# Delta rule: chunk outputs and the samples' r in 128 by 32 parts of the array

## The chip, the cores and the metric

The kernel runs on one core of a Trainium2 chip. The metric is the device time of one execution in microseconds: before the change 1140.02 us, median of three runs (1139.94 to 1140.26). Engines are named as in the profile: PE (TensorE, matrix products), PEld (its weight loads), DVE (VectorE), ACT (ScalarE), POOL (GpSimd), SP (SyncE, which issues the transfers here).

## What is computed

One layer of a hybrid decoder, in float32, over 256 prompt tokens and 64 sample tokens (8 sequences of 8), 320 together. One projection of the normed input (2048 by 12,416) feeds two branches. Branch B is a gated linear recurrence with 8 heads. Branch A is RWKV-7: 16 heads of 64, each with a 64 by 64 state that follows a delta rule per token:

```
sa  = S kk
S   = S diag(w) - sa (kk * a)^T + v k^T
y_t = S r_t
```

Then come a group norm over each head, a bonus term, gates, two projections (1024 by 2048), a merge by sigmoid gates, and an output projection (2048 by 2048) with a final norm. States and outputs of the prompt and of all sequences are returned.

## The kernel before, in words

**Stages.** A start (30 us) norms and transposes the input. The *planned part* (30 to 702 us) runs the input projection, 128 output columns at a time over 320 tokens, together with both branches, two heads of A (a *pair*, `rwkv`, p = 0 to 7) and one of B (`hgrn`) for each of eight rounds. Then the gates' columns and `proj_a`, `proj_b` (from 702 us), and `w_out` with the norm.

**Weight products.** A weight matrix is divided into two parts of the type fp32r (ACT copies, DVE subtracts), the input too, and three products per 128 by 128 block go into the PSUM tile `mps`. They make the *stream*. All other products are small; most are float32, and the trace shows two records (passes) for each of these.

**The planner.** In the planned part every call is recorded (`Recorder`), linked by what it reads and writes, and issued in an order that a model of the engines gives (`order`, line 209 on). On PE a small product that is ready is put between stream products. Each operation has a cost (line 126 on), so other tile shapes and other counts move everything that follows. Products recorded by `side_by_side` are one *group*: they inherit each other's inputs, so none is issued before all inputs of the group are there. A product on fewer than 128 rows or columns of the array has its own `mode`; the planner stays in a mode while it has work for it (a *visit*), and counts a cost for going in and out. The instructions of the planned part all carry line 1435 in the profile (1441 in the changed kernel), so groups are told apart by tiles.

**The delta rule** (`rwkv`, line 780 on) takes the prompt in four chunks of 64 tokens, both heads in one 128 by 128 block. `arp` holds the decayed kk and r by key, `bk2` and `bk` the decayed keys, `uv` the vectors u (or v) by token, `g2` the masked products of keys with kk and r, `yz`/`ys` the inverted triangles, `s0t` the samples' states (key by value, four tiles of two sequences). Two generators run in turns. `chunks` does for each chunk: the right side (`pr`), u (`pu`), the state's step (`pd`, then `st`), and the output into the PSUM tile `y`: the state times r, and u times the masked products. These are seven products of 128 by 128 with 128 columns, of which the 64 by 64 blocks on the diagonal are used. `samples` does the same for the 64 sample tokens: four products of `s0t` with `arz`, which has kk and r of both heads with zeros elsewhere; a copy of the kk part (`sr0`), turned by a product with the identity and added to `g2` times `uv` (`pr2`); u; the output `py2`, added on DVE to the r part (`sr1`); and the states' step in a visit of four 64 by 64 parts (`pd2`, tile `big` in the profile). `yh` and `yl` are the two fp32r parts of the output, which the group norm reads (`jr_cent`, `jr_mean`).

**The group of branch B** (`pos`, `pg`) is 42 products of 128 rows by 32 columns of the array: eight with 128 columns of moving data, four with 64, the others with 32; one visit a round.

Of the kernel before, what the change touches and what calls it, by code (L numbers as in the profile page):

```python
# [9 lines left out]
F32 = mybir.dt.float32  # L10
F32R = mybir.dt.float32r
# [6 lines left out]
NP_ = 256  # L18
NS = 64
NT = NP_ + NS  # L20
# [274 lines left out]
def hybrid_step(ctx, tc, x_prompt, x_sample, state_rwkv, state_hgrn, state_shift, norm_g, w_in,  # L295
# [4 lines left out]
    V, S, G, T = nc.vector, nc.scalar, nc.gpsimd, nc.tensor  # L300
# [17 lines left out]
    ident = ctile([128, 128], "ident", pool=const)  # L318
# [15 lines left out]
    HS = [slice(0, 64), slice(64, 128)]  # L334
# [29 lines left out]
    def run(gen):  # L364
        for _ in gen:
            pass
# [9 lines left out]
    with tc.tile_pool(name="start", bufs=1) as st, \  # L376
# [167 lines left out]
        with tc.manual_schedule(engines={mybir.EngineType.PE, mybir.EngineType.Activation, mybir.EngineType.DVE,  # L544
# [16 lines left out]
            arp = ctile([128, 5, 2, 2, 64], "arp")  # L561
# [14 lines left out]
            for c_ in range(4):  # L576
                ps = pst.tile([128, 512], F32, name="gps", tag="t")
# [80 lines left out]
            ps = pst.tile([128, 512], F32, name="cps", tag="t")  # L658
# [47 lines left out]
    def ring(pool, tag, shape, bufs, dt, size, clear=False):  # L706

        if (pool.name, tag) not in rings:
            n_ = size or math.prod(shape[1:])
            rings[pool.name, tag] = [0, [pool.tile([128, n_], dt, name=f"{tag}_{j}", tag=f"{tag}_{j}")  # L710
                                         for j in range(bufs)]]
            for t_ in rings[pool.name, tag][1]:
                if clear:
                    G.memset(t_ if dt == F32 else t_.bitcast(F32), 0.0)
        r_ = rings[pool.name, tag]
        t_ = r_[1][r_[0] % len(r_[1])]
        r_[0] += 1
        t_ = t_[:shape[0], :math.prod(shape[1:])]
        if len(shape) == 2:
            return t_  # L720
        names = "abcdef"[:len(shape) - 1]
        return t_.rearrange(f"p ({' '.join(names)}) -> p {' '.join(names)}", **dict(zip(names, shape[1:])))
# [2 lines left out]
             "w1": 384, "w2": 320, "w3": 320, "ks": 128, "ket": 256, "o": NT}  # L725


    CLEAR = {"uB", "uE", "ys", "rhs", "rhs2", "k3", "vm", "w1", "vt", "att", "attc"}
# [9 lines left out]
    def aps(name="aps"):  # L738
        return ring(psa, "a", [128, 512], 3, F32, None)
# [2 lines left out]
        return ring(psb, "b", [128, 512], 2, F32, None)  # L742

    def parts(src, tile_=at):
        hi, lo = tile_("rh", dt=F32R), tile_("rl", dt=F32R)
        S.copy(hi, src)
        V.tensor_sub(lo, src, hi.bitcast(F32))
        return hi, lo
# [31 lines left out]
    def rwkv(p, r, k, vp, za):  # L780
        c = lambda base: cols[:, base + p:base + p + 1]
        v = vp[:, 64:]
# [84 lines left out]
        ps = aps("ps0")  # L867
# [10 lines left out]
                         bk2[:, 4, :, 32 * a_:32 * a_ + 32].rearrange("p j (s i) -> p j s i", i=8),  # L878
                         f[:, None, 8 + 4 * a_:12 + 4 * a_, None].to_broadcast([128, 2, 4, 8]))

        arz = at("arz", (128, 4, 2, 2, 2, 8))
        G.memset(arz, 0.0)
        for h in range(2):
            for s_ in range(2):
                src = arp[HS[h], 4, :, h].rearrange("p x (a b i) -> p b a x i", b=2, i=8)
                G.tensor_copy(arz[HS[s_], :, s_, h], src[:, s_])


        g2 = at("g2", (128, 5, 2, 2, 64))
# [115 lines left out]

        def chunks():
            st_ = None
            py = ring(psy, "y", [128, 512], 1, F32, None)  # L1010
            for ci in range(4):
                cp, c_ = ci // 2, ci % 2
                tk = HS[c_]
                ps = aps("pr")
                T.matmul(ps[:, :128], g2[:, ci, 0].rearrange("p h t -> p (h t)"), uv[:, ci].rearrange("p h v -> p (h v)"), start=True, stop=st_ is None)
                if st_ is not None:
                    T.matmul(ps[:, :128], arp[:, ci, 0].rearrange("p h t -> p (h t)"), st_, start=False, stop=True)
                rt = at("rhs", (128, 2, 64))
                V.tensor_copy(rt[tk, 0], ps[HS[0], 0:64])
                S.copy(rt[tk, 1], ps[HS[1], 64:128])  # L1020
                yield
                pu = aps("pu")
                T.matmul(pu[:, :128], yz[:, cp, c_].rearrange("p h t -> p (h t)"), rt.rearrange("p h t -> p (h t)"), start=True, stop=True)
                V.tensor_scalar(uv[tk, ci, 0], pu[HS[0], 0:64], -1.0, 0.0, op0=ALU.mult, op1=ALU.add)
                S.activation(uv[tk, ci, 1], pu[HS[1], 64:128], AF.Copy, scale=-1.0)
                yield
                pd = aps("pd")
                T.matmul(pd[:, :128], bk[:, ci], uv[:, ci].rearrange("p h v -> p (h v)"), start=True, stop=True)
                sn = at("st", (128, 128), bufs=2)
                fc = f[:, 4 + ci:5 + ci]  # L1030
                if st_ is None:
                    V.tensor_scalar(sn, pd[:, :128], fc, 0.0, op0=ALU.mult, op1=ALU.add)
                else:
                    V.scalar_tensor_tensor(sn, pd[:, :128], fc, sf, op0=ALU.mult, op1=ALU.add)
                po = py[:, 128 * ci:128 * ci + 128]
                if st_ is not None:
                    T.matmul(po, st_, arp[:, ci, 1].rearrange("p h t -> p (h t)"), start=True, stop=False)
                T.matmul(po, uv[:, ci].rearrange("p h v -> p (h v)"), g2[:, ci, 1].rearrange("p h t -> p (h t)"), start=st_ is None, stop=True)
# [12 lines left out]
            so = at("so", (64, 2, 64))  # L1051
            for h in range(2):
                S.copy(so[:, h], ps[HS[h], 64 * h:64 * h + 64])
            Y.dma_start(p_rwkv[0, 0, 2 * p:2 * p + 2].rearrange("h v k -> v h k"), so)
            yield


        def samples():
            ps = aps("psr")
            for sp in range(4):  # L1060
                T.matmul(ps[:, 64 * sp:64 * sp + 64], s0t[:, sp], arz[:, sp].rearrange("p b h x i -> p (b h x i)"),
                         start=True, stop=True)

            sr0, sr1 = at("sr0", (128, 2, 64)), at("sr1", (128, 64))
            for h in range(2):
                p4 = ps[HS[h], :256].rearrange("p (s h x i) -> p h x s i", h=2, x=2, i=8)[:, h]
                V.tensor_copy(sr0[HS[h]].rearrange("p h (s i) -> p h s i", i=8),
                              p4[:, 0:1].to_broadcast([64, 2, 8, 8]))
                S.copy(sr1[HS[h]].rearrange("p (s i) -> p s i", i=8), p4[:, 1])
            yield  # L1070
            ps = aps("pr2")
            T.matmul(ps[:, :128], sr0.rearrange("p h t -> p (h t)"), ident, start=True, stop=False)
            T.matmul(ps[:, :128], g2[:, 4, 0].rearrange("p h t -> p (h t)"), uv[:, 4].rearrange("p h v -> p (h v)"), start=False, stop=True)

            uh = at("uh", (128, 128), tag="s0t")
            for a_ in range(2):
                S.copy(uh[64 * a_ + 32:64 * a_ + 64], uv[64 + 32 * a_:96 + 32 * a_, 4].rearrange("p h v -> p (h v)"))
            rhs = at("rhs2", (128, 2, 64))
            V.tensor_copy(rhs[0:64, 0], ps[HS[0], 0:64])
            S.copy(rhs[0:64, 1], ps[HS[1], 64:128])  # L1080
# [26 lines left out]
            T.matmul(py[:, :128], uv[:, 4].rearrange("p h v -> p (h v)"), g2[:, 4, 1].rearrange("p h t -> p (h t)"), start=True, stop=True)  # L1107
# [4 lines left out]
            yield  # L1112
# [11 lines left out]
            yield  # L1124

        run(together(chunks(), samples()))


        ps = aps("pyc")
# [487 lines left out]
```

## Time and profile before

| | |
|---|---|
| runs | 1140.02 us (1139.94 to 1140.26) |
| profiled execution | 1139.92 us, of which span 1138.2 us |
| PE / PEld / DVE / ACT / POOL busy | 1122.0 / 1087.7 / 766.8 / 700.7 / 179.8 us |
| granted clock of PE | 0.998 |
| read from HBM, written | 148.53 MB, 9.81 MB |

A row of a group reads: line, engine, operation, tile written <- tiles read, rows*columns of the array, moving data, type, count; then busy us, mean ns of one, and idle time of the engine before them. Matmuls are pipelined and overlap in the records; their durations don't add up to the time that they take. A row of the timeline has start and duration in us, and ends with how many records were put together in it. A wait's row has its sum in us, how often, and the longest.

### The profile page before, as it was taken

How to read it: one execution, taken by the hardware profiler on the slowest of the kernel's cores; microseconds unless marked ns; L12 is line 12 of the kernel's file. 1: busy time of each engine (PE TensorE's matmuls, PEld its weight loads, DVE VectorE, ACT ScalarE, POOL GpSimd, SP SyncE). 2: the span in 40 equal slices, each digit the busy share in tenths (PEclk: the TensorE clock that was granted, in tenths of full speed). 3: DMA queues.
4: the chain of work that ended last, by engine and by line, in shares of the span. 5: the costliest groups of instructions: out<-in, count | busy, mean ns of one | idle time of the engine just before them, and what ended most of it. 6: DMA issues, size and time to landing. Idle time of an engine off the chain costs nothing.

```text
span 1138.2 us, 21837 instructions
## 1 busy us (share of the span) xinstructions
PE 1122.0 (99%) x8312; PEld 1087.7 (96%) x8312; DVE 766.8 (67%) x1634; ACT 700.7 (62%) x1612; POOL 179.8 (16%) x385
## 2 busy tenths in 40 slices
PE   7999999999999999999999999999999999999997
PEld 6999999999999999999999999999999999988886
DVE  8878788787887887888778877444444444437532
ACT  6667767777678677678667777444444444435422
POOL 9531132122221411311312200000000000000000
PEclk9999999999999999999999999999999999999999
DMA  6744544535435445345436345555555555587512
GB/s 182 192 114 112 154 115 129 150 95 146 132 100 154 130 114 144 106 111 159 123 96 168 99 122 145 155 148 149 149 149 149 150 149 153 151 272 258 161 38 93
DMA packets 283101, 159.76 MB, mean 140 GB/s; under 512 B 22893, under 2 KB 273264, under 8 KB 282356
## 3 DMA queue, kind: packets, MB, share of 16 engines
q1 hardware_dynamic: 282996, 158.37, 48.7%
q8 instruction: 65, 1.06, 0.4%
q14 instruction: 40, 0.33, 0.1%
HBM read 148.53 MB, written 9.81 MB: 139 GB/s over the span
## 4 chain that ended last, share of the span: by engine, by line
PE 98%; DVE 1%; POOL 0%; ACT 0%; issue 0%; ACTq 0%; DVEq 0%; POOLq 0%
PE mps L1435 42%; PE a L1435 12%; PE mps L359 6%; PE mps L360 6%; PE mps L361 6%; PE b L1435 3%; PE po L1518 3%; PE po L1519 3%; PE po L1520 3%; PE ppb L359 2%; PE ppa L359 2%; PE ppb L360 2%; PE ppa L360 2%; PE ppb L361 2%; PE ppa L361 2%; PE po L1524 1%
## 5 line engine op out<-in xcount | busy, mean ns | idle before, releaser
L1435 PE MATMUL mps<-hhi,whi 128*128 128x320 f32 x1088 | 345.4, 317 | 0.0
L1435 PE MATMUL mps<-hlo,whi 128*128 128x320 f32 x1088 | 345.3, 317 | 0.0
L1435 PE MATMUL mps<-hhi,wlo 128*128 128x320 f32 x1088 | 343.8, 316 | 0.0
L1435 PEld LDWEIGHTS mps<-hhi,wlo 128*128 128x128 f32 x1088 | 204.9, 188 | 2.4 <-issue 1.5
L1435 PEld LDWEIGHTS mps<-hlo,whi 128*128 128x128 f32 x1088 | 205.0, 188 | 1.4 <-issue 0.8
L1435 PEld LDWEIGHTS mps<-hhi,whi 128*128 128x128 f32 x1088 | 204.9, 188 | 1.1 <-issue 0.4
L349 ACT CAST whi<-raw 128x1024 fp32r<-128x1024 f32 x88 | 92.4, 1050 | 162.8 <-PE mps L360 107.3
L350 DVE TENSOR_TENSOR wlo<-raw,whi 128x1024 fp32r<-128x1024 f32 x88 | 107.9, 1226 | 125.0 <-ACT whi L349 124.8
L1435 ACT CAST whi<-raw 128x1024 fp32r<-128x1024 f32 x134 | 140.4, 1048 | 66.3 <-PE mps L1435 65.4
L1435 DVE TENSOR_TENSOR wlo<-raw,whi 128x1024 fp32r<-128x1024 f32 x134 | 166.6, 1243 | 18.1 <-ACT whi L1435 16.7
L359 PE MATMUL mps<-hhi,whi 128*128 128x320 f32 x448 | 138.4, 309 | 0.0
L360 PE MATMUL mps<-hlo,whi 128*128 128x320 f32 x448 | 138.4, 309 | 0.0
L361 PE MATMUL mps<-hhi,wlo 128*128 128x320 f32 x448 | 138.4, 309 | 0.0
L359 PEld LDWEIGHTS mps<-hhi,whi 128*128 128x128 f32 x448 | 84.1, 188 | 0.0
L360 PEld LDWEIGHTS mps<-hlo,whi 128*128 128x128 f32 x448 | 84.1, 188 | 0.0
L361 PEld LDWEIGHTS mps<-hhi,wlo 128*128 128x128 f32 x448 | 84.1, 188 | 0.0
L1507 DVE TENSOR_TENSOR wlo<-raw,whi 128x1024 fp32r<-128x1024 f32 x32 | 38.7, 1223 | 39.0 <-ACT whi L1506 39.0
L1506 ACT CAST whi<-raw 128x1024 fp32r<-128x1024 f32 x32 | 33.5, 1053 | 49.0 <-PE po L1523 32.0
L1518 PE MATMUL po<-whi,mhi 128*128 128x512 f32 x128 | 50.1, 391 | 0.7 <-DVE gbt L1475 0.7
L1519 PE MATMUL po<-whi,mlo 128*128 128x512 f32 x128 | 50.0, 391 | 0.0
L1520 PE MATMUL po<-wlo,mhi 128*128 128x512 f32 x128 | 50.0, 391 | 0.0
L359 PE MATMUL ppa<-yah,whi 128*128 128x320 f32 x128 | 39.6, 309 | 0.0
(428 smaller groups left out, 2268.6 us busy)
## 6 DMA issues: line engine op xcount, KB each, us to landing
raw<-in_w_in_dram SPq DMA_DIRECT2D x194, 512.0 KB
raw<-in_w_out_dram SPq DMA_DIRECT2D x32, 512.0 KB
raw<-in_proj_a_dram SPq DMA_DIRECT2D x16, 512.0 KB
raw<-in_proj_b_dram SPq DMA_DIRECT2D x16, 512.0 KB
s<-in_state_hgrn_dram SPq DMA_DIRECT2D x8, 512.0 KB
out_dram<-s SPq DMA_DIRECT2D x8, 512.0 KB
s<-in_state_rwkv_dram SPq DMA_DIRECT2D x8, 256.0 KB
out_dram<-s SPq DMA_DIRECT2D x8, 256.0 KB
```

The costliest lines, as they stand in the source:

```text
L349: S.copy(hi[:, ks], raw[:, ks])
L350: sub.tensor_sub(lo[:, ks], raw[:, ks], hi[:, ks].bitcast(F32))
L359: T.matmul(dst, hi[:, q, :], xhi[:, k, :], start=(k == 0), stop=False)
L360: T.matmul(dst, hi[:, q, :], xlo[:, k, :], start=False, stop=False)
L361: T.matmul(dst, lo[:, q, :], xhi[:, k, :], start=False, stop=(k == nk - 1))
L1435: o.fn(*o.args, **o.kw)
L1506: S.copy(hi, raw)
L1507: V.tensor_sub(lo, raw, hi.bitcast(F32))
L1518: T.matmul(pt, h, hi, start=first, stop=False)
L1519: T.matmul(pt, l, hi, start=False, stop=False)
L1520: T.matmul(pt, h, lo, start=False, stop=end)
L1524: T.matmul(pt, h, lo, start=False, stop=end)
```

## The change

It makes the same sums in other places.

- The zero-padded `arz` becomes two tiles: `az` has kk of the samples, by head and half of the tokens, for use as the stationary operand, and `rz` has r. POOL fills them with eight copies a pair; the zeros are set once, when the tiles are made (`CLEAR`).
- The samples' right side is made in one group of twelve products, each 128 rows by 32 columns of the array with 64 columns of moving data: four parts (head, half of the tokens), and for each of them two with the states and one with `g2` and `uv`. `sr0`, `sr1`, the turn by the identity and `py2` are gone.
- The chunks keep their states (`st` has four buffers), and the outputs of all chunks and of the samples are made after both generators, in one group of 48 products into the tile `y`, 128 rows by 32 columns each: 32 with 64 columns (the samples' u among them) and 16 with 16 columns (states times `rz`). The four parts are head and half of its 64 value rows, so no block off the diagonal is made.
- `yh` and `yl` are made by one copy and one subtraction over 320 tokens instead of three of each. `uh` is made later, in the buffer of `rhs2`; `s0t` is kept to the last visit. Branch B's `rh` takes the buffer of `vm`.

```diff
-    CLEAR = {..., "vt", "att", "attc"}
+    CLEAR = {..., "vt", "att", "attc", "az", "rz"}
...
-        hi, lo = tile_("rh", dt=F32R), tile_("rl", dt=F32R)
+        hi, lo = tile_("rh", tag="rh" if tile_ is at else "vm", dt=F32R), tile_("rl", dt=F32R)
...
-        arz = at("arz", (128, 4, 2, 2, 2, 8))
-        G.memset(arz, 0.0)
+        az = at("az", (128, 2, 2, 96))
+        rz = at("rz", (128, 4, 2, 2, 8))
         for h in range(2):
             for s_ in range(2):
-                src = arp[HS[h], 4, :, h].rearrange("p x (a b i) -> p b a x i", b=2, i=8)
-                G.tensor_copy(arz[HS[s_], :, s_, h], src[:, s_])
+                own = arp[HS[h], 4, :, h]
+                G.tensor_copy(az[HS[s_], h].rearrange("p a (e f) -> p a e f", f=48)[:, :, :, 8 * s_:8 * s_ + 8],
+                              own[:, 0].rearrange("p (a e b i) -> p a e b i", a=2, e=2, b=2)[:, :, :, s_])
+                G.tensor_copy(rz[HS[s_], :, h, s_], own[:, 1].rearrange("p (a b i) -> p a b i", b=2, i=8)[:, :, s_])
...
         def chunks():
-            py = ring(psy, "y", [128, 512], 1, F32, None)
...
-                sn = at("st", (128, 128), bufs=2)
+                sn = at("st", (128, 128), bufs=4)
...
-                po = py[:, 128 * ci:128 * ci + 128]
-                if st_ is not None:
-                    T.matmul(po, st_, arp[:, ci, 1]..., start=True, stop=False)
-                T.matmul(po, uv[:, ci]..., g2[:, ci, 1]..., start=st_ is None, stop=True)
                 st_ = sn
+                states.append(sn)
...
-            for h in range(2):
-                t4 = lambda t_: t_[HS[h], :NP_].rearrange("p (c t) -> p c t", t=64)
-                y4 = py.rearrange("p (c h t) -> p c h t", c=4, h=2)[HS[h], :, h]
-                S.copy(t4(yh), y4)
-                V.tensor_sub(t4(yl), y4, t4(yh).bitcast(F32))
...
         def samples():
             ps = aps("psr")
-            for sp in range(4):
-                T.matmul(ps[:, 64 * sp:64 * sp + 64], s0t[:, sp], arz[:, sp]..., start=True, stop=True)
-            sr0, sr1 = at("sr0", (128, 2, 64)), at("sr1", (128, 64))
-            for h in range(2):
-                p4 = ps[HS[h], :256].rearrange("p (s h x i) -> p h x s i", h=2, x=2, i=8)[:, h]
-                V.tensor_copy(sr0[HS[h]]..., p4[:, 0:1].to_broadcast([64, 2, 8, 8]))
-                S.copy(sr1[HS[h]]..., p4[:, 1])
-            yield
-            ps = aps("pr2")
-            T.matmul(ps[:, :128], sr0..., ident, start=True, stop=False)
-            T.matmul(ps[:, :128], g2[:, 4, 0]..., uv[:, 4]..., start=False, stop=True)
+            work = []
+            for step in range(3):
+                for h in range(2):
+                    for a_ in range(2):
+                        l_, r_ = (az[:, h, a_, 32 * step:32 * step + 32], s0t[:, 2 * a_ + step, 64 * h:64 * h + 64]) \
+                            if step < 2 else (g2[:, 4, 0, h, 32 * a_:32 * a_ + 32], uv[:, 4, h])
+                        o_ = 64 * h + 32 * a_
+                        work.append(((ps[o_:o_ + 32, :64], l_, r_), dict(start=step == 0, stop=step == 2)))
+            side_by_side(work)
...
-            py = aps("py2")
-            T.matmul(py[:, :128], uv[:, 4]..., g2[:, 4, 1]..., start=True, stop=True)
-            for h in range(2):
-                V.tensor_add(sr1[HS[h]], py[HS[h], 64 * h:64 * h + 64], sr1[HS[h]])
-            S.copy(yh[:, NP_:], sr1)
-            V.tensor_sub(yl[:, NP_:], sr1, yh[:, NP_:].bitcast(F32))
...
         run(together(chunks(), samples()))
+        py = ring(psy, "y", [128, 512], 1, F32, None)
+        work = []
+        parts4 = [(h, 64 * h + 32 * w, w) for h in range(2) for w in range(2)]
+        for ci in range(5):
+            cols_ = slice(64 * ci, 64 * ci + 64)
+            if 0 < ci < 4:
+                for h, o_, w in parts4:
+                    work.append(((py[o_:o_ + 32, cols_], states[ci - 1][:, o_:o_ + 32], arp[:, ci, 1, h]),
+                                 dict(start=True, stop=False)))
+            for h, o_, w in parts4:
+                work.append(((py[o_:o_ + 32, cols_], uv[:, ci, h, 32 * w:32 * w + 32], g2[:, ci, 1, h]),
+                             dict(start=ci in (0, 4), stop=ci < 4)))
+        for sp in range(4):
+            for h, o_, w in parts4:
+                t_ = NP_ + 16 * sp
+                work.append(((py[o_:o_ + 32, t_:t_ + 16], s0t[:, sp, o_:o_ + 32], rz[:, sp, h]...),
+                             dict(start=False, stop=sp == 3)))
+        side_by_side(work)
+        S.copy(yh, py[:, :NT])
+        V.tensor_sub(yl, py[:, :NT], yh.bitcast(F32))
```

How it moves instructions on PE is shown at three places of the last pair. The names: `a_`, `b_` and `y_` are PSUM tiles, `s_0_519` and `s_0_520` branch B's states, `w`, `o`, `ket`, `ks` its decayed queries and keys, `st` the chunks' states. First, PE of the kernel before, in the middle of the chunks:

```order
L1435 MATMUL a_488<-fd_516,jr_sum 128x256
L1435 MATMUL a_487<-rhs_0_510,ys_502 128x128
L1435 MATMUL b_523<-vm_538,k_0_537 128x512
L1435 MATMUL a_486<-uv_495,g_0_501 128x128
L1435 MATMUL a_486<-st_511,arp 128x128
L1435 MATMUL y_506<-arp,st_511 128x128
L1435 MATMUL a_488<-fd_516,jr_sum 128x256
L1435 MATMUL a_487<-g_0_501,uv_495 128x128
```

The output of a chunk (`y_506`) stands beside the next chunk's right side, and the last row is the samples' output `py2`, both on the whole array, between other small products. In the changed kernel, PE after the last chunk of the same pair:

```order
L1441 MATMUL a_487<-uv_495,bk_504 128x128
L1441 MATMUL y_519<-g_0_502,uv_495 32x64 x4
L1441 MATMUL y_519<-arp,st_512 32x64 x4
L1441 MATMUL y_519<-g_0_502,uv_495 32x64 x4
L1441 MATMUL y_519<-arp,st_513 32x64 x4
L1441 MATMUL y_519<-g_0_502,uv_495 32x64 x4
L1441 MATMUL y_519<-arp,st_514 32x64 x4
L1441 MATMUL y_519<-g_0_502,uv_495 32x64 x8
L1441 MATMUL y_519<-rz_501,s0t_497 32x16 x16
L1441 MATMUL mps<-hhi,wlo 128x320
```

All outputs of the pair now stand here as one block of 48 products, behind the last state's product, with the stream on both sides; so it is in each of the eight pairs. The third place is the visit for the samples' right side, PE of the changed kernel, same pair:

```order
L1441 MATMUL b_523<-s_0_520,qz 32x128 x8
L1441 MATMUL b_524<-w_0_529,w_0_521 32x32 x8
L1441 MATMUL b_524<-w_0_528 32x32 x8
L1441 MATMUL b_524<-o_531 32x32 x8
L1441 MATMUL b_524<-ket_532 32x32 x4
L1441 MATMUL b_524<-ks_534,s_0_533 32x64 x4
L1441 MATMUL b_524<-w_0_529,w_0_521 32x32 x2
L1441 MATMUL a_487<-s0t_497,az_500 32x64 x8
L1441 MATMUL a_487<-uv_495,g_0_502 32x64 x4
```

The last two rows are the twelve new products; here, and in the fourth pair, they stand in one visit with branch B's group, in the other six pairs by themselves. The states' visit (`big`) stands in one visit with branch B's in four pairs of the changed kernel and in three before. The variance's product (`jr_mean`) of the last pair has two more stream products ahead of it than before.

More of the change, by code (lines that the diff above doesn't have):

```diff
@@ L725, in hybrid_step @@
              "w1": 384, "w2": 320, "w3": 320, "ks": 128, "ket": 256, "o": NT}
-    CLEAR = {"uB", "uE", "ys", "rhs", "rhs2", "k3", "vm", "w1", "vt", "att", "attc"}
+    CLEAR = {"uB", "uE", "ys", "rhs", "rhs2", "k3", "vm", "w1", "vt", "att", "attc", "az", "rz"}
     def at(name, shape=(128, NT), tag=None, bufs=1, dt=F32):
@@ L1003, in rwkv @@
         yl = at("yl", tag="rl", dt=F32R)
+        states = []
         def chunks():
             st_ = None
-            py = ring(psy, "y", [128, 512], 1, F32, None)
             for ci in range(4):
@@ L1034, in chunks @@
                     V.scalar_tensor_tensor(sn, pd[:, :128], fc, sf, op0=ALU.mult, op1=ALU.add)
-                po = py[:, 128 * ci:128 * ci + 128]
-                if st_ is not None:
-                    T.matmul(po, st_, arp[:, ci, 1].rearrange("p h t -> p (h t)"), start=True, stop=False)
-                T.matmul(po, uv[:, ci].rearrange("p h v -> p (h v)"), g2[:, ci, 1].rearrange("p h t -> p (h t)"), start=st_ is None, stop=True)
                 st_ = sn
+                states.append(sn)
                 if ci < 3:
@@ L1059, in samples @@
             ps = aps("psr")
-            for sp in range(4):
-                T.matmul(ps[:, 64 * sp:64 * sp + 64], s0t[:, sp], arz[:, sp].rearrange("p b h x i -> p (b h x i)"),
-                         start=True, stop=True)
-            sr0, sr1 = at("sr0", (128, 2, 64)), at("sr1", (128, 64))
-            for h in range(2):
-                p4 = ps[HS[h], :256].rearrange("p (s h x i) -> p h x s i", h=2, x=2, i=8)[:, h]
-                V.tensor_copy(sr0[HS[h]].rearrange("p h (s i) -> p h s i", i=8),
-                              p4[:, 0:1].to_broadcast([64, 2, 8, 8]))
-                S.copy(sr1[HS[h]].rearrange("p (s i) -> p s i", i=8), p4[:, 1])
-            yield
-            ps = aps("pr2")
[L1072 to L1077, printed above, removed]
+            work = []
[7 more added lines that the diff above has]
+            side_by_side(work)
             rhs = at("rhs2", (128, 2, 64))
-            V.tensor_copy(rhs[0:64, 0], ps[HS[0], 0:64])
-            S.copy(rhs[0:64, 1], ps[HS[1], 64:128])
+            V.tensor_copy(rhs[0:64, 0], ps[HS[0], :64])
+            S.copy(rhs[0:64, 1], ps[HS[1], :64])
             yield
@@ L1105, in samples @@
             yield
-            py = aps("py2")
-            T.matmul(py[:, :128], uv[:, 4].rearrange("p h v -> p (h v)"), g2[:, 4, 1].rearrange("p h t -> p (h t)"), start=True, stop=True)
-            for h in range(2):
-                V.tensor_add(sr1[HS[h]], py[HS[h], 64 * h:64 * h + 64], sr1[HS[h]])
-            S.copy(yh[:, NP_:], sr1)
-            V.tensor_sub(yl[:, NP_:], sr1, yh[:, NP_:].bitcast(F32))
-            yield
+            uh = at("uh", (128, 128), tag="rhs2")
+            for a_ in range(2):
+                S.copy(uh[64 * a_ + 32:64 * a_ + 64], uv[64 + 32 * a_:96 + 32 * a_, 4].rearrange("p h v -> p (h v)"))
             for a_ in range(2):
@@ L1126, in rwkv @@
         run(together(chunks(), samples()))
+        py = ring(psy, "y", [128, 512], 1, F32, None)
[13 more added lines that the diff above has]
+                t_ = NP_ + 16 * sp
+                work.append(((py[o_:o_ + 32, t_:t_ + 16], s0t[:, sp, o_:o_ + 32], rz[:, sp, h].rearrange("p b i -> p (b i)")),
+                             dict(start=False, stop=sp == 3)))
+        side_by_side(work)
+        S.copy(yh, py[:, :NT])
+        V.tensor_sub(yl, py[:, :NT], yh.bitcast(F32))
         ps = aps("pyc")
```

## The prediction, made before the changed kernel ran

> **What bounds the kernel now.** I read the page's busy table first, then the chain, then the stages.
>
> ```profile
> span 1138.2 us, 21837 instructions
> PE 1122.0 (99%) x8312; PEld 1087.7 (96%) x8312; DVE 766.8 (67%) x1634; ACT 700.7 (62%) x1612; POOL 179.8 (16%) x385
> PE 98%; DVE 1%; POOL 0%; ACT 0%; issue 0%; ACTq 0%; DVEq 0%; POOLq 0%
> 230.00:330.00 100.00, 100.00 (x815) 98.42 (x814) 82.65 (x208) 74.10 (x196) 23.41 (x49) 1.00 0.45 124
> 530.00:630.00 100.00, 99.69 (x810) 97.50 (x809) 82.63 (x202) 70.29 (x181) 23.89 (x53) 1.00 0.47 128
> ```
>
> The last two rows are stages of the planned part: window, its length, then busy time of PE, weight loads, DVE, ACT, POOL, the granted clock, the DMA share and GB/s. PE has no gap, its clock is 1.00, DVE is busy for 83 of 100 us. PE alone decides here: an instruction saved on PE is time saved, and one saved elsewhere is not. But "busy" is no price, because matmuls overlap. The price of a product is by how much it pushes the next start, and that is read from the timeline of PE. This is the last head pair, around its samples (columns: start, duration, instruction, count):
>
> ```profile
> 662.58 0.31 PE L1435 MATMUL mps<-hhi,whi 128*128 128x320 f32 x1
> 662.73 1.00 PE L1435 MATMUL a<-arz,s0t 128*128 128x64 f32 x8
> 663.56 0.44 PE L1435 MATMUL a<-rhs,yz 128*128 128x128 f32 x2
> ...
> 663.99 0.31 PE L1435 MATMUL mps<-hhi,wlo 128*128 128x320 f32 x1
> ...
> 664.58 0.31 PE L1435 MATMUL mps<-hhi,whi 128*128 128x320 f32 x1
> 664.81 0.65 PE L1435 MATMUL b<-s,qz 128*32 128x128 f32 x16
> 665.27 0.31 PE L1435 MATMUL b<-w,w 128*32 128x32 f32 x16
> ...
> 665.67 0.20 PE L1435 MATMUL b<-ket 128*32 128x32 f32 x1
> ...
> 665.77 0.30 PE L1435 MATMUL b<-ks,s 128*32 128x64 f32 x6
> 665.86 0.24 PE L1435 MATMUL b<-w,w 128*32 128x32 f32 x4
> 666.03 0.41 PE L1435 MATMUL mps<-hlo,whi 128*128 128x320 f32 x1
> 666.28 0.38 PE L1435 MATMUL a<-ident,sr 128*128 128x128 f32 x2
> 666.50 0.27 PE L1435 MATMUL b<-ident,es 128*64 128x128 f32 x1
> 666.61 0.39 PE L1435 MATMUL a<-uv,g 128*128 128x128 f32 x2
> 666.83 0.39 PE L1435 MATMUL a<-uv,bk 128*128 128x128 f32 x2
> 667.05 0.39 PE L1435 MATMUL y<-g,uv 128*128 128x128 f32 x2
> 667.20 0.39 PE L1435 MATMUL mps<-hhi,wlo 128*128 128x320 f32 x1
> 667.43 0.31 PE L1435 MATMUL mps<-hhi,whi 128*128 128x320 f32 x1
> ```
>
> Each float32 product stands as two records (passes). The stream of weight products (mps) runs at one per 0.147 us: 663.99 to 664.58 are four. The four products of `arz` run from 662.73 to 663.56, 0.83 us. `ident,sr` takes 666.28 to 666.50, `uv,g` 666.61 to 666.83: 0.22 us each. `y<-g,uv` runs from 667.05; one stream product starts inside it (667.20) and the next at 667.43, so 0.38 less 0.147, 0.23 us.
>
> **Removed.** How many such products there are is in the groups of PE (count, then busy us, mean ns of one):
>
> ```profile
> L1435 PE MATMUL y<-g,uv 128*128 128x128 f32 x64 | 12.4, 275 | 0.0
> L1435 PE MATMUL y<-arp,st 128*128 128x128 f32 x48 | 9.3, 275 | 0.0
> L1435 PE MATMUL a<-arz,s0t 128*128 128x64 f32 x64 | 8.1, 267 | 0.0
> L1435 PE MATMUL a<-uv,g 128*128 128x128 f32 x80 | 15.5, 275 | 0.0
> L1435 PE MATMUL a<-g,uv 128*128 128x128 f32 x16 | 3.1, 274 | 0.0
> L1435 PE MATMUL a<-ident,sr 128*128 128x128 f32 x16 | 3.1, 273 | 0.0
> ```
>
> By pair these are four and three products into `y`, four of `arz`, one of `sr`, one of `g,uv` into `py2`, and of the ten records of `uv,g` the two of the samples (the other eight are the chunks' and stay). So ten products of 128 columns go at 0.22, 2.20 us, and the four of `arz` at 0.83: 3.03 us a pair, **24.2 us** over eight. The busy column would promise 39.1 us (12.4 + 9.3 + 8.1 + 3.1 + 3.1 and a fifth of 15.5); the rest of that lies under neighbours.
>
> **Added: passes of 128 by 32 parts.** The trace has this form in branch B's visit. Sixteen passes with 128 columns take 664.81 to 665.27, 28.75 ns each. 46 passes with 32 columns take 665.27 to 665.67, 8.7 ns each. Six with 64 columns take 665.77 to 665.86, 15 ns each; half of 28.75 is 14.4. I take 14.5 ns for 64 columns. The ends are 8.7, the row below it, and 28.75, the row above. For 16 columns there is no row: I take 8.7, what 32 columns cost, since fewer columns can't cost more; the other end is half of it.
>
> The last visit has 32 products with 64 columns and 16 with 16, that is 64 and 32 passes: 0.93 + 0.28 = 1.21 us. The visit for r has 12 products with 64 columns, 24 passes: 0.35 us.
>
> **Added: going in and out.** Branch B's visit: the stream would have gone on at 664.58 + 0.147 = 664.73, the first pass starts at 664.81. The last four passes start at 665.86 and take 0.03; the stream starts at 666.03, but its next instruction comes at 666.28, 0.25 later instead of 0.147. In and out are 0.08 + 0.24, 0.32 us. The state's visit of four 64 by 64 parts, in an earlier pair, gives the same:
>
> ```profile
> 186.46 0.30 PE L1435 MATMUL mps<-hlo,whi 128*128 128x320 f32 x1
> 186.70 0.66 PE L1435 MATMUL a<-big,s0t 64*64 64x256 f32 x8
> 187.29 0.41 PE L1435 MATMUL mps<-hhi,wlo 128*128 128x320 f32 x1
> 187.54 0.31 PE L1435 MATMUL mps<-hhi,whi 128*128 128x320 f32 x1
> ```
>
> From 186.46 + 0.147 to 187.54 - 0.147 are 0.79 us; eight passes with 256 columns at twice 28.75 are 0.46; 0.33 is left. I take 0.33 for a visit, with 0.08 (the way in alone) and 0.45 (a third more, an estimate) as ends.
>
> By the order of the changed kernel the last visit stands alone in all eight pairs: 8 x (1.21 + 0.33) = 12.3 us. The visit for r stands alone in six; in the fourth and the last pair it is joined to branch B's visit of the same form, and pays no way in or out: 8 x 0.35 + 6 x 0.33 = 4.8 us. The state's visit joins branch B's in four pairs now, in three before; the forms differ, so I count 0.2 of 0.33 saved. Added: 12.3 + 4.8 - 0.2 = **16.9 us**.
>
> **Other engines.** DVE loses six instructions a pair and ACT four; both lie under the stream and are worth nothing. POOL loses a memset and four copies and gets eight:
>
> ```profile
> L1435 POOL COPY arz<-arp x32: 231/268/1135, 62.3 to 623.5; 64x64 f32<-64x64 f32 x32
> L1435 POOL MEMSET arz<- x8: 305/311/312, 37.0 to 573.6; 128x256 f32 x8
> ```
>
> Eight at 0.27 (half the elements each, so at most that) less four and 0.31 are 0.8 us a pair more. Behind them on POOL stand the first blocks `yz` of the inverse, so that chain starts up to 0.8 us later; the stream of weight products covers it. If that cover were gone, it would be 6 us in all. No DMA is added or moved.
>
> **Waits.** A visit is issued as one block and waits for all of its inputs: the last one for the state after the third chunk, u of the fourth and the samples' u. Behind a late input stands the whole weight stream. Against this, what PE waited for in this stage, of everything the planner has placed, is one row:
>
> ```profile
> PE a L1435 <- DVE st L1435: 0.3, 1, 0.3
> ```
>
> I take 0 for the sixteen visits; 0.46 each would cost the whole gain (7.3 / 16).
>
> The outputs of the last pair now come out in one piece after the last chunk, with the norm and the projections behind them. Room there:
>
> ```profile
> L1455 ACT CAST yah<-ya x4: 712/717/724, 696.5 to 699.1; 128x640 fp32r<-128x640 f32 x4
> L1456 DVE TENSOR_TENSOR yal<-ya,yah x4: 817/822/825, 697.5 to 700.0; 128x640 fp32r<-128x640 f32 x4
> L359 PE MATMUL ppa<-yah,whi x128: 309/309/309, 709.3 to 1008.0; 128*128 128x320 f32 x128
> ```
>
> The last split ends at 700.8, PE asks for it at 709.3: 8.5 us. In the order the variance's product of the last pair stands two stream products later than before, 0.3 us. Nothing.
>
> **Sum.** 24.2 - 16.9 = 7.3 us. The profiled execution took 1139.92 us (span 1138.2 and 1.7 around it), 0.1 below the runs' median of 1140.02. 1139.92 - 7.3 = 1132.6; I say **1132.5 us**.
>
> **Rivals.** (1) *A pass with 64 columns costs more than in branch B's visit*, 20 to 25 ns, because here nearly all passes have 64 and in that visit only eight do, among passes with 32. There are 8 x (64 + 24) = 704: 5.5 ns more are 3.9 us, 10.5 more 7.4: 1136.5 to 1140.0. For it: six passes are little to read a pitch from. Against it: 128 columns at 28.75.
>
> (2) *A pass has a floor whatever its columns*, 28.75 ns by the nearest row with long moving data. The 120 passes of a pair then cost 3.45 us, with the ways in and out 27.6 + 4.6 - 0.2 = 32.0 us against 24.2: 1147.7, slower. It decides from about 20.6 ns a pass (24.2 - 4.4 = 19.8 us over 960). Against it stand 46 passes at 8.7 ns. The Trainium skill, page "TensorE: Matmul & The Clock Gate", section "Wait — 56ns, not 53.3ns?", states such a floor: start-to-start never under about 25 ns however small N is. By it the 960 passes would be 24.0 us and the time 1139.9 + 24.0 + 4.4 - 24.2 = 1144.1, slower. The trace disagrees with it for passes that go to different column groups: 8.7 ns.
>
> (3) *The visits wait.* The weight stream stands behind a visit whose inputs come late; at 0.9 us for each of sixteen, 14.4 us, 1147, slower; from 0.46 each there is no gain left. For it: the planner works with costs of its own, and the last visit's inputs come off three engines. Against it: the 0.3 us above, which is all for eight pairs of small products.
>
> (4) *The parts don't overlap where they accumulate.* Two or five products add into one place here; branch B's tiles are single products. A pass that had to wait for the end of the one before it (some 0.22 us) at about nine places a pair would cost 16 us: 1148. Against it: the two passes of one product already add into one place, and pass each other at that pitch.
>
> **How the numbers follow.** A gain of 4.4 to 11 us (1129 to 1135.5): 0.80. (1), with a gain of 0 to 4.4: 0.11. (2): 0.02. (3): 0.05. (4): 0.02. The range goes from 1129.5, where the passes with 64 columns cost 11 ns (2.5 us less) and a few old stalls go, to 1136.5, where they cost 20; that leaves out some 0.17. What this kernel's measurement can tell from no change is about 0.2%, 2.3 us. Faster by more: 0.80 and 0.08 of (1), 0.88. Within it: 0.04. Slower: (2), (3) and (4) with little else, 0.08.
>
> **What would show it.** In the timeline of the changed kernel: the last visit's 96 passes start within 1.2 us and the next stream product is running 0.3 us after; the visit for r takes 0.35 us. The groups of `arz`, `sr` and `y` at 128 by 128 are gone. The planned part, which ends near 702 us, ends near 695; what comes after takes as long as before. The forecast is wrong if the 64-column passes start over 20 ns apart, or if PE's waits in this stage sum to more than 3 us.

## The result, and the profile after

The changed kernel takes 1133.64 us (median of six runs, 1133.14 to 1134.63), the kernel before 1139.97 beside it: 6.3 us less, ratio 0.9945 (95% interval 0.9932 to 0.9958). The forecast was 1132.5, range 1129.5 to 1136.5. The profiled execution took 1133.88 us, 6.0 less than that of before.

The page of the changed kernel, and the rows of the stream's last kind (first and last start):

```profile
span 1132.1 us, 23282 instructions
PE 1110.7 (98%) x9048; PEld 1072.6 (95%) x9048; DVE 754.8 (67%) x1586; ACT 691.3 (61%) x1580; POOL 193.9 (17%) x411
L1441 PE MATMUL mps<-hhi,wlo x1088: 302/309/502, 29.6 to 695.6; 128*128 128x320 f32 x182
```

PE has more records (9048 for 8312) and is busy for less time. The planned part ends near 696 instead of 702 us (the prediction had 695). The last visit of the last pair, in the timeline of PE:

```profile
677.63 0.31 PE L1441 MATMUL mps<-hlo,whi 128*128 128x320 f32 x1
677.77 0.38 PE L1441 MATMUL a<-uv,bk 128*128 128x128 f32 x2
678.09 0.32 PE L1441 MATMUL y<-g,uv 128*32 128x64 f32 x8
678.22 0.29 PE L1441 MATMUL y<-arp,st 128*32 128x64 f32 x8
...
678.78 0.41 PE L1441 MATMUL y<-g,uv 128*32 128x64 f32 x16
679.00 0.47 PE L1441 MATMUL y<-rz,s0t 128*32 128x16 f32 x32
679.40 0.41 PE L1441 MATMUL mps<-hhi,wlo 128*128 128x320 f32 x1
679.65 0.27 PE L1441 MATMUL a<-ident,st 128*128 128x128 f32 x1
```

64 passes with 64 columns start between 678.09 and 679.00: 14.2 ns each. The 32 passes with 16 columns run from 679.00; the stream's product after them is there at 679.40, with the way out. After `uv,bk` (0.22 from 677.77) the first pass comes 0.1 later. In all, 677.99 to 679.65 less 0.147 are 1.51 us; the prediction had 1.54. The visit for r in the first pair:

```profile
92.24 0.31 PE L1441 MATMUL mps<-hhi,whi 128*128 128x320 f32 x1
92.48 0.43 PE L1441 MATMUL a<-s0t,az 128*32 128x64 f32 x16
92.73 0.29 PE L1441 MATMUL a<-uv,g 128*32 128x64 f32 x8
92.95 0.42 PE L1441 MATMUL mps<-hlo,whi 128*128 128x320 f32 x1
93.21 0.49 PE L1441 MATMUL b<-ident,i 128*128 128x128 f32 x3
```

From 92.39 (92.24 + 0.147) to 93.21 less 0.147 are 0.67 us, for a predicted 0.68. What did not come as predicted are the waits. These are PE's in the planned part of the changed kernel, as the profile lists them; the kernel before had one row there, the 0.3 us that the prediction quotes:

```profile
PE a L1441 <- POOL fd L1441: 1.7, 1, 1.7
PE a L1441 <- DVE ast L1441: 1.0, 1, 1.0
```

The list leaves out short waits. To see the whole of the planned part, I took the times between stretches of undisturbed stream and split them by the prices: stream and whole-array products (0.147 a stream product, 0.1105 a float32 pass), what a visit takes beyond that, and the rest as waits (us; the later rows are experiments told below):

```
kernel                         stream and whole array   visits   waits   sum
before                                          639.7     29.2     2.4  671.4
changed                                         614.9     46.3     4.5  665.8
only the outputs in parts                       625.6     40.8     2.2  668.6
only the samples' r in parts                    636.1     33.9     2.0  672.1
outputs twice in one visit                      614.9     70.2     2.5  687.7
outputs twice, apart                            614.9     58.5     5.5  678.9
outputs of 128 columns                          614.9     54.4     2.4  671.7
two buffers for fd                              614.9     49.5     1.3  665.7
two buffers, at most 64 products a visit        614.9     47.5     1.3  663.8
the same, 30 stream products apart              614.9     45.7     1.5  662.2
one buffer, 64 products, 30 apart               614.9     46.4     5.3  666.6
```

24.8 us of whole-array products are gone (forecast 24.2), 17.1 us of visits came (16.9), and the waits grew by 2.1 us (forecast 0): the planned part is 5.6 us shorter. In this count the wait for `fd` makes 1.9 us, that for `ast` 1.1, and all other waits together are 0.9 less than before.

The wait for `ast` is not the change's doing. The start was 0.86 us shorter in this profile than in that of before (the first eight records of `tps<-ident,xt` took 0.71 us for 1.11), so PE came to this product 0.86 us earlier and had to wait for its input. The last experiment, which leaves the change out, has the shorter start and a wait for `ast` too. `w_out` took 0.4 us longer: its first product starts 6.4 us earlier than before, its last 6.0. So the 6.0 us between the two profiles are 5.6 of the planned part and 0.86 of the start, less 0.4 of `w_out`.

### The profile page after: what moved, and what is told of

Read it like the earlier page. It is cut to its first block, busy times and chain, and to the rows that moved or that the text cites. A ratio compares the mean times of both kernels' runs of the same rounds, so it can differ in the third digit from the quotient of the medians.

```text
span 1132.1 us, 23282 instructions
## 1 busy us (share of the span) xinstructions
PE 1110.7 (98%) x9048; PEld 1072.6 (95%) x9048; DVE 754.8 (67%) x1586; ACT 691.3 (61%) x1580; POOL 193.9 (17%) x411
## 4 chain that ended last, share of the span: by engine, by line
PE 89%; DMA 3%; DVE 3%; issue 3%; ACT 1%; POOL 1%; ACTq 0%; SPq 0%; POOLq 0%; DVEq 0%
PE mps L1441 40%; PE a L1441 11%; PE mps L360 6%; PE mps L361 6%; PE mps L359 6%; PE b L1441 3%; DMA raw<-in_w_out_dram 2%; PE po L1526 2%; PE po L1524 2%; PE po L1525 2%; PE ppb L360 2%; PE ppa L361 2%; PE ppa L360 2%; PE ppa L359 2%; PE ppb L359 2%
```

## The experiments

**One group at a time.** First, the samples' right side as before, the outputs in parts:

```diff
-        az = at("az", (128, 2, 2, 96))
+        arz = at("arz", (128, 4, 2, 2, 2, 8))
...
-            side_by_side(work)
+            # four products with arz, sr0, its turn by ident, g2 times uv
```

> One of the two groups undone: the samples' right side is made as before (four products with arz, the turn by the identity, g2 times uv, all on the whole array), the group of 48 output products stays. Theory (PE's time is the sum of what its products and visits occupy): against the kernel before, 8 x 8 x 0.22 = 14.1 us of whole-array outputs go, 8 x 1.21 = 9.7 come, and by the order there are 18 visits instead of 13, 5 x 0.33 = 1.7: 1137 to 1138 us, so the group of outputs alone gains some 2.5 us and the group for r the larger rest (4 us). Rival (the groups don't matter, the new order of the planner does): anything between 1132 and 1140, with no relation to the sum. Rival (a pass with 64 columns costs 20 to 25 ns): 1140 to 1143.

1136.47 us (1136.30 to 1136.82), ratio 0.9970 (0.9959 to 0.9982): 3.4 us below before, where the sum gave 2.7, and 0.5 below the range expected. The start is the shorter one here too (0.84 us); the planned part alone is 2.8 us shorter. Then the other way round, the outputs on the whole array and the twelve products for r kept:

```diff
-        rz = at("rz", (128, 4, 2, 2, 8))
+        arz = at("arz", (128, 4, 2, 2, 8))
...
-        side_by_side(work)
+            # seven products into y in chunks(); in samples() four with arz, and py2
```

> The other group undone: outputs of chunks and samples as before on the whole array, the group of twelve for the samples' right side stays. The states times r then need four whole-array products of 32 columns again. Theory: against the kernel before, two products of 0.22 a pair go (3.5 us), 8 x 0.35 = 2.8 come, and by the order there are 18 visits instead of 13 (1.7 us): about 1141 us, no gain at all, if a whole-array product of 32 columns takes the 0.21 us that one of 64 takes; if it takes in proportion to its columns, 3.3 us less, 1137.7. The gain of the change is then not the sum of its halves: the four products of arz go only when both groups are there. Rival (each group is worth its half): about 1137.

1140.65 us, ratio 1.0008 (0.9999 to 1.0017): no gain, as the sum said with 0.21 us for a whole-array product of 32 columns. Its rows:

```profile
L1442 PE MATMUL a<-arz,s0t 128*128 128x32 f32 x64 | 7.8, 265 | 0.0
L1442 PE MATMUL a<-s0t,az 128*32 128x64 f32 x128 | 3.8, 223 | 0.0
```

There are 64 passes of `arz` again, half as wide and nearly as long (7.8 us for 8.1). The halves are worth 3.4 and -0.8 us and the whole 6.3: with one group alone the four products of `arz` stay, and only both together free PE of them. Without the start and the waits, by the first two columns of the table, the halves are worth 2.5 and -1.1 us and the whole 7.7, for sums of 2.7, -1.0 and 7.3. The rival, a new order of the planner with no relation to the sum, would not give that.

**The passes.** The group of 48 twice in one visit:

```diff
-        side_by_side(work)
+        side_by_side(work + work)
```

> The group of 48 output products is issued twice in one visit, with the same result: the visit's passes alone are doubled, not its way in and out. Theory: 64 passes at 14.3 ns and 32 at 9 are 1.21 us a pair, 9.7 in all, and two more visits by the order (0.6): 1143 to 1145 us. Rival (a pass with 64 columns costs 20 ns or more): 1146 or more. Rival (a floor of 25 to 29 ns for every pass): 1153 to 1156.

1155.66 us, ratio 1.0142 (1.0128 to 1.0156). The theory missed by over 10 us. The number lies in the range of the rival with a floor of 25 to 29 ns for every pass, but the timeline of PE shows no such floor. In the second pair:

```profile
197.90 0.32 PE L1441 MATMUL y<-g,uv 128*32 128x64 f32 x8
...
199.76 0.44 PE L1441 MATMUL y<-g,uv 128*32 128x64 f32 x16
199.98 0.29 PE L1441 MATMUL y<-rz,s0t 128*32 128x16 f32 x13
203.54 0.36 PE L1441 MATMUL y<-rz,s0t 128*32 128x16 f32 x19 [3.27 <-issue]
203.83 0.42 PE L1441 MATMUL mps<-hlo,whi 128*128 128x320 f32 x1
```

The first 160 passes start within 2.1 us, up to 199.98, at the pitch of the changed kernel (128 at 14.2 ns and 32 at 9 ns). 13 more follow, and then PE stands for 3.3 us with nothing to wait for (`issue`). The waits of this kind in this kernel:

```profile
PE y L1441 <- issue: 8.0, 4, 3.3
PE b L1441 <- issue: 1.5, 1, 1.5
```

Three of the eight visits had no stop. They last 2.47, 2.49 and 2.63 us up to the next product on the whole array, where the changed kernel's take 1.31: there the second copy cost 1.2 to 1.3 us, as expected (1.21). Of the 23.9 us that the table's visits hold more than the changed kernel's, 9.7 are these passes, 0.6 two more visits and 9.5 the stops of the list. Most of the rest, 3 us by an estimate, are two stretches of some 3.5 us behind a stop, in which a stream product took 0.267 us for 0.147 (see the last section).

At the time of the stop instructions were being loaded. The trace's records of PE's instruction queue have one transfer of 16,384 bytes for some 256 instructions; those around the stop, with the number of PE's instructions (passes and weight loads) that started since the transfer before:

```
transfer, us from start    PE instructions since the one before
181.21 to 182.34           285
186.92 to 188.10           241
200.96 to 201.89           509
205.09 to 205.96            50
```

With stream products 256 instructions last 19 us (two for each 0.147 us). A visit uses as many in under 2 us, and in no kernel here do two transfers start less than 3.4 us apart. The stop above ends 1.65 us after the transfer that ends at 201.89, and so it is with all ten stops of this kind in the traces here: PE goes on 1.3 to 1.7 us after such a transfer is complete. That made a new theory, *a burst of short instructions uses them up faster than they come*, and two tests. The first has as many instructions in a longer visit, with 128 columns of moving data in 28 of the 32 products that had 64:

```diff
-            cols_ = slice(64 * ci, 64 * ci + 64)
+            wide = 128 if ci < 4 else 64
+            cols_ = slice(64 * ci, 64 * ci + wide)
...
```

> As many instructions as in the changed kernel, but 28 of the 48 output products get 128 columns of moving data instead of 64 (the second half is overwritten by the next chunk's product or not read), so that the visit lasts longer. In the kernel with the outputs twice, PE stopped inside the long visits for 1.4 to 3.4 us with nothing to wait for in the profile, 3.4 us while one 16 KB block of instructions was being fetched. Theory (PE runs out of instructions: a burst of short ones uses them up faster than the next block comes): a longer visit with the same instructions costs its passes alone, 56 x 14.3 ns x 8 = 6.4 us more than the changed kernel, 1139.5 to 1140.5, and no stop over 1 us. Rival (PE stops when it has been in a visit for long): stops as in the kernel with the outputs twice, 1146 or more.

1139.83 us (1138.91 to 1141.04), in the range of the theory, but partly by luck. Seven of the visits take 0.75 us longer (2.06 for 1.31) and none of them stops, as the theory said. The eighth, which the planner joined to branch B's group, stops for 1.9 us, and the expectation had no stop over 1 us. Against that, this order has no wait for `fd`, another 1.9 us that the expectation did not count on; the two cancel. The second test has the copy in its own visit, where the planner leaves a visit rather than pass 64 products in it (the rule is shown below):

```diff
-    APART, MARGIN, WAIT, OVER = 10, 250, 6000, 130
+    APART, MARGIN, WAIT, OVER = 30, 250, 6000, 130
...
         V.tensor_sub(yl, py[:, :NT], yh.bitcast(F32))
+        side_by_side(work)
```

> The outputs twice again, as many passes as in the kernel with the group doubled (1155.7 us), but the second copy in a visit of its own, at least 30 stream products (4.4 us) after the first; the planner keeps 30 stream products between any two visits and no more than 64 products in one. Theory (instructions run out in a long burst, and come again in time where bursts are apart): the passes 9.7 us and nine more visits at 0.33: 1144 to 1147 us, some 10 us under the kernel with the group doubled. Rival (the second copy is dear by itself): 1153 or more.

1146.67 us, ratio 1.0060 (1.0045 to 1.0076), 9 us under the other kernel with as many passes. No wait for `issue` stands in PE's list. So the passes cost 14 and 9 ns, and what a burst costs beyond them hangs on how many instructions stand close together. The number in one visit does not decide alone: besides the three visits of 96 products above, one of 90 products in the kernel with only the outputs in parts had no stop either.

**The waits.** In the changed kernel's first pair PE waits for the second of two tiles `fd`:

```profile
94.27 0.28 PE L1441 MATMUL a<-fd,jr_sum 128*128 128x256 f32 x1
94.63 2.57 POOL L1441 TENSOR_TENSOR fd<-id,fq 128x256 fp32r<-128x256 f32 x1 [22.01 <-PE a L1441]
94.77 1.21 DVE L1441 TENSOR_TENSOR wlo<-raw,whi 128x1024 fp32r<-128x1024 f32 x1
97.25 0.39 PE L1441 MATMUL a<-fd,jr_sum 128*128 128x256 f32 x1 [1.68 <-POOL fd L1441]
```

POOL may not write it until PE has read the first (one buffer), and takes 2.57 us, where the median of these is 0.62. The two products are no closer than in other places: without the wait the second would stand 1.1 to 1.3 us behind the first, as it does in the other seven pairs, which have no wait. What differs is POOL's time. In all kernels here, whenever POOL took over 1.3 us for an `fd`, a subtraction `wlo` ran on DVE beside it, as in the third row; but other `fd` beside a `wlo` took 0.62, and what decides between the two stays open.

```diff
-                fd = at("fd", (128, NSEQ, 32), dt=F32R)
+                fd = at("fd", (128, NSEQ, 32), tag=("fd", "rh")[hf], dt=F32R)
```

> The second of the two tiles fd (POOL makes them for the samples' decay, PE sums them) gets a buffer of its own, that of rh, so that POOL need not wait for PE's first product before it makes the second. In the changed kernel's first pair PE waits 1.7 us for the second fd. Theory (that wait is a gap in the sum and goes with its cause): 1131 to 1132.3 us, faster than the changed kernel by about 1.7. Rival (the planner's order shifts and another wait takes its place): 1133 to 1135.

1134.72 us (1133.02 to 1135.33), 0.9954 (0.9940 to 0.9967): no faster than the changed kernel, though the wait is gone: in the table the waits are 3.2 us less and the visits 3.2 more. The planner's order shifted, and joined the outputs' visit with branch B's in one round:

```profile
584.30 0.45 PE L1441 MATMUL y<-rz,s0t 128*32 128x16 f32 x31
...
585.47 0.20 PE L1441 MATMUL b<-ket 128*32 128x32 f32 x1
587.97 0.23 PE L1441 MATMUL b<-ket 128*32 128x32 f32 x3 [2.30 <-issue]
```

The same stop, in a visit of 90 products. A limit of 64 products moves that one group:

```diff
...
+                fits = lambda o: o.mode == (128, 128) or o.group == visit[1] or visit[0] + sizes.get(o.group, 1) <= 64
+                if mode != (128, 128) and any(map(fits, can)):
+                    own, part, can = ([o for o in c if fits(o)] for c in (own, part, can))
...
```

> The kernel with two buffers for fd (1134.7 us median, where PE stopped for 2.5 us in the one visit that joins the outputs with branch B's group, 90 products), and one rule more in the planner: a visit holds no more than 64 products. By the order this moves one thing alone: branch B's group of that round comes ten stream products later. Theory (instructions run out): the stop goes, 0.33 for a visit more comes: 1132 to 1133. Rival (order makes no difference): 1134 to 1135.

1132.21 us (1131.50 to 1132.84), 0.9933 (0.9920 to 0.9945), 2.5 us less in the median; between the profiled executions, 1133.39 and 1132.21, it is 1.2. Branch B's group in that round, now apart:

```profile
587.70 0.20 PE L1449 MATMUL b<-o 128*32 128x32 f32 x1
588.07 0.29 PE L1449 MATMUL b<-o 128*32 128x32 f32 x11 [0.17 <-issue]
```

0.2 is left of 2.3; a stop of 0.5 in a visit of 48 products is in both kernels. With 30 stream products between visits as well:

```diff
-    APART, MARGIN, WAIT, OVER = 10, 250, 6000, 130
+    APART, MARGIN, WAIT, OVER = 30, 250, 6000, 130
```

> As the kernel before it in this list, and 30 stream products between two visits instead of 10, so that a block of instructions (3.6 to 4 us from one fetch to the next at the shortest) comes between two bursts. Theory (instructions run out): also the small stops go, 1131 to 1132.3, and the runs spread less than the 2.3 us of the kernel with two buffers alone. Rival: no difference from that one, 1133 to 1135.

1130.11 us (1129.85 to 1130.73), ratio 0.9915 (0.9902 to 0.9929), the fastest version: 9.8 us under the kernel before and 3.5 under the changed one. Two more kernels ask which part of it does what: the limit and the 30 stream products on the changed kernel with its one buffer, and on the kernel before.

> The changed kernel with the planner's rule alone (30 stream products between two visits, no more than 64 products in one), one buffer for fd as it was. Theory (of the gap between forecast and result, part is the supply of instructions): under the changed kernel's 1133.6 by what the small stops take, and the 1.7 us wait for the second fd stays if the order around it stays: 1131.5 to 1133, with a narrow spread of runs (under 1 us, where the changed kernel has 1.5). Rival (all of the gain of the best version is the buffer of fd): 1133 to 1135.

1134.41 us (1134.32 to 1134.45), 0.9952 (0.9939 to 0.9964): no faster. Here the theory missed. Its wait list has the 1.7 us for `fd` as before, and the table shows 5.3 us of waits against 1.5 with the second buffer. What it had right is the spread of the runs, 0.13 us where the changed kernel has 1.5.

> The kernel before with the planner's rule alone, as a control. There only branch B's group and the states' step are visits, 92 products a round, and no stop shows in them. Theory (the rule is worth something only where there are many short instructions): 1139 to 1141, no change. Rival (the best version's gain over the changed kernel is the planner's order and has nothing to do with the visits): 1136 to 1138.

1139.29 us, 0.9995 (0.9986 to 1.0004): nothing, where visits are few. (Its start is the shorter one, 0.84 us; its planned part is as long as before.) So the rule and the second buffer gain 4.6 and 4.3 us when the other is there, and nothing alone. Of the 4.3, 1.9 are `fd`'s and 0.7 the visits'; most of the rest are waits of 0.2 to 0.3 us at small products, and why one order has fewer of them than the other stays open.

## Why the prediction was right

- **PE alone decides.** Right: with the start and the waits set aside, the changed kernel and its two halves follow the sum of PE's products and visits to within 0.4 us, and no wait of PE points to the 48 instructions less on DVE or the 32 less on ACT. Another engine did count in one place, POOL at `fd`.
- **Removed, 24.2 us** by the next start instead of busy time: 24.8. The busy column's 39.1 would have forecast some 22 us of gain.
- **Passes.** 14.5 ns with 64 columns were 14.2; 8.7 with 16 were 9, so fewer columns did cost a little more than the 8.7 of 32. The ends named (8.7 and 28.75) were far out, and the choice by half of the row above was right. Rivals 1 and 2 fall with this. The Trainium skill's floor of about 25 ns from start to start ("TensorE: Matmul & The Clock Gate", section "Wait — 56ns, not 53.3ns?") is not there for passes that go round four column groups. Rival 4 falls too: parts that add into one place run at the same pitch.
- **Way in and out, 0.33 us** for 13 more visits: the two shown took 1.51 and 0.67 in all, for 1.54 and 0.68.
- **Waits, taken as 0.** This is the step that was off: the table's waits grew by 2.1 us. The change's own part of that is the 1.9 us at `fd`; the 1.1 at `ast` came with the shorter start, and other waits fell by 0.9. They were not at the visits, as rival 3 had it, but at a small product whose input POOL made in 2.57 us instead of 0.62, beside other work on DVE than before; what of it slowed POOL is not shown. The prediction looked for what the change delays and not for what a new order brings side by side on other engines. It also read the waits from the list, 0.3 us, where the table finds 2.4 us of short ones. Its sign of being wrong, waits of more than 3 us, was not reached by the list, which has 2.7; the table has 4.5, with 2.4 of them there before. POOL's eight copies, the tail after the last pair and the outputs' split cost nothing that shows.
- **The total.** The forecast's gain was 7.4 us, the measured one 6.3. Between the profiles, 24.8 - 17.1 gives 7.7; less 2.1 of waits and 0.4 of `w_out`, and with 0.86 of a shorter start, it is 6.0. The start had no place in the forecast, so part of the closeness is luck. The planned part of the best version is 9.2 us shorter than before: 24.8 - 16.5, and 0.9 of waits less than before. A start shorter by 0.8 makes that 10.0 between the profiles, and 9.8 between the medians.

## What to carry to other kernels

Where one engine is busy throughout, price an instruction by how much it pushes the next start, and count by the order; here the two sums held to 3 per cent. What they leave out are waits that a reordering makes anywhere. So look after the change at single buffers that tie this engine to another: here the other engine took four times as long for one instruction, beside other work. Check also that the parts of the program that were not changed take as long in both profiles. Products of which only a part is used are worth packing into parts of the array when a visit has many of them: here the way in and out costs as much as 23 passes with 64 columns. Keep bursts of short instructions small and apart: in visits of 90 products and more PE could run out of instructions.

## What the runs showed of the hardware that was not expected

PE can stop for lack of instructions. It stopped for 1.2 to 3.3 us in seven of the eleven visits of 90 products and more (two passes each, every pass with its weight load), and not, or for at most 0.5 us, in the other visits, of 54 products and fewer. Each time it went on 1.3 to 1.7 us after a block of instructions had landed. The Trainium skill, "Runtime: NRT & Kernel Launch", section "Instruction fetch mechanics", says that instructions come in blocks of 16 KiB, and the transfers here agree; it also says that fetching is hidden because instructions are issued more slowly than they come, and these stops disagree.

After the longest stop PE was slow for a while. Windows of the kernel with the outputs twice (window, length, busy PE, PEld, DVE, ACT, POOL, granted clock, DMA share, GB/s):

```profile
190.00:197.00 7.00, 7.00 (x54) 6.94 (x53) 4.79 (x11) 5.76 (x19) 0.29 (x1) 1.00 0.71 195
204.00:208.00 4.00, 4.00 (x18) 4.00 (x19) 0.89 (x2) 2.07 (x7) 0.00 (x0) 0.57 0.05 12
```

The granted clock is 0.57 behind the stop of 3.3 us, and 1.00 ahead of it. The same kernel shows 0.57 once more, from 446 to 450 us, behind a stop of 2.06 us. But a stop of 2.3 us, in the kernel with two buffers, left the clock at 1.00:

```profile
588.57 0.31 PE L1441 MATMUL a<-yh,jr_cent 128*128 128x320 f32 x1
...
589.38 0.30 PE L1441 MATMUL mps<-hhi,whi 128*128 128x320 f32 x1
589.52 0.31 PE L1441 MATMUL mps<-hlo,whi 128*128 128x320 f32 x1
```

These stream products start 0.14 us apart as ever. So the length of the stop alone does not decide, and what does stays open.
